# Attention scores as one full product and two 64-row products in different halves of the array

## The chip, the cores and the metric

The kernel runs on one core of a Trainium2 chip. The metric is the device time of one execution in microseconds, the median of several runs. The engines are named as in the profile: PE is TensorE (matrix products; PEld its weight loads), DVE is VectorE, ACT is ScalarE, POOL is GpSimd, and SP is SyncE, whose queue (SPq) issues most DMAs.

## What is computed

One layer of an encoder on 2048 tokens of width 1024, in float32:

```
h  = rms_norm(x); z = h @ W_in -> q_A k_A v_A q_B k_B v_B gate_A gate_B
yA = windowed attention, |t-s| <= 128, 8 query heads on 2 key heads, ALiBi, a sink logit per head
yB = attention in an 8 x 16 neighbourhood of a 32 x 64 token grid, 8 heads, learned bias
x  = x + (sigmoid(gate_A) * (yA @ Wp_A) + sigmoid(gate_B) * (yB @ Wp_B)) @ W_out
x  = x + relu(rms_norm(x) @ W_up)^2 @ W_down
out = rms_norm(x)
```

The head dimension is 64. The scores of both attentions are q . k over these 64 numbers, plus a bias, then a softmax.

## The kernel before

Every float32 operand of a product is split into a rounded high part and a low part (the rest), both in the type float32r. Dense products are three: high times high, high times low, low times high (`mm3`, L199, and `mm3s`, L296).

Scores use another scheme. As a head has only 64 rows, q is stored with its high part in rows 0 to 63 and its low part in rows 64 to 127. The keys are kept twice: once as (high; low) in `k[:, 0]`, once swapped, as (low; high) in `k[:, 1]`. Two products of 128 rows, added in one PSUM bank, then give all four combinations of high and low:

```
PE.matmul(ps[:, :n], q[:, h, :], ka[:, 0, ...], start=True, stop=False)    # L764: hh + ll
PE.matmul(ps[:, :n], q[:, h, :], ka[:, 1, ...], start=False, stop=True)    # L765: hl + lh
```

The stages, in order of time:

- W_in for the first half of the tokens (`in_quad`), with results sent to DRAM. `qk_parts` (L426) splits a result into its parts and returns where they go; the q and k scratch in DRAM are `qs_a`, `qs_b`, `ks_a`, `ks_b`. L464 issues these stores here, L705 for the other half of the tokens, one DMA for each head with both parts.
- Attention A (`attn_a`, L747), 32 units: 2 key heads by 16 blocks of 128 queries. A unit loads its q (L757), makes the scores of 4 heads against up to 384 keys (L764, L765), adds the bias and takes the maximum on DVE (L766), then exponentials on ACT, normalisation on POOL, transposes on PE (L784), and products with v (L789, L790). `load_kv` (L739) loads the keys (L742 to L744).
- Attention B (`attn_b`, L909), 32 units: 8 heads by 4 stripes of columns. A unit has 4 blocks of 128 queries with 288, 384 or 512 keys (L927, two products each), DVE (L932), and the like (transposes at L955, products with v at L967). `load_k` (L900) loads the keys of a head in three DMAs (L904 to L906).
- Between the units of both, the dense products of W_in for the other half of the tokens stand as filler (`feature_tile`, L200 to L202, in `mm3`).
- Then the projections, W_out, the up product and the down product.

PSUM has eight banks in the attention stages: two for `mm` (dense), three for `s` (scores), two for `pt` (transposes), one for `av`. A score takes the next of the three `s` banks and holds it until the DVE pass at L766 or L932 has read it. The order on each engine isn't written out by hand: a scheduler sets it from the dependencies, its estimate of times, and the order in which the program emits the instructions; `issue_after` adds an order by hand in some places, not at the scores.

Of the kernel before, what the change touches and what calls it, by code (L numbers as in the profile page):

```python
# [8 lines left out]
F32 = mybir.dt.float32  # L9
# [13 lines left out]
P = 128  # L23
KC = D // P
NB = 4
BT = 512
# [8 lines left out]
B_R0 = [0, 4, 12, 20]  # L35
B_NR = [12, 16, 16, 12]
B_C0 = [0, 8, 24, 40]
# [55 lines left out]
def encoder_layer(ctx, tc, x, norm_mix, w_in, b_gate, sink, rpb, w_pa, w_pb, w_out,  # L93
                  norm_mlp, w_up, w_down, norm_final, dist_a, mask_b, out):
    nc = tc.nc
    V, A, G, PE, SY = nc.vector, nc.scalar, nc.gpsimd, nc.tensor, nc.sync
# [21 lines left out]
    def psum(tag, bufs):  # L118
        n_ps[0] += 1
        return pps[tag].tile([P, 512], F32, tag=tag, bufs=bufs, name=f"{tag}_{n_ps[0]}")  # L120
# [20 lines left out]
    def flipped(t):  # L141

        (step, n), _ = t.ap
        return bass.AP(t.tensor, t.offset + P - 1, [[step, n], [P, 4], [-16, 8], [-1, 16]])
# [26 lines left out]
    def flush(keep=0, queue=A):  # L171
        while len(pending) > keep:
            queue.dma_start(*pending.pop(0))
# [152 lines left out]
    def zbank(pl, bufs=1):  # L326
        n_ps[0] += 1
        return pl.tile([P, 512], F32, tag="b", bufs=bufs, name=f"zb_{n_ps[0]}")
# [97 lines left out]
    def qk_parts(col, b, src, t2):  # L426

        th, tl = t2[:, 0], t2[:, 1]
        if O_QB <= col < O_VB:
            if col < O_KB:  # L430

                pv = src.rearrange("p (r j c) -> p j r c", r=8, j=4)
                hv, hr, lr = (flipped(t) for t in (th, th.bitcast(F32R), tl.bitcast(F32R)))
            else:

                pv = src.rearrange("p (q r x) -> p q r x", q=2, r=4)
                hv, hr, lr = (t.rearrange("p (q x r) -> p q r x", q=2, r=4)
                              for t in (th, th.bitcast(F32R), tl.bitcast(F32R)))
            A.copy(hr, pv)
            V.tensor_tensor(out=lr, in0=pv, in1=hv, op=ALU.subtract)  # L440
        else:
            scale = 1.0 if col == O_KA else 0.125
            A.activation(th.bitcast(F32R), src, AF.Copy, scale=scale)
            last_low[0] = V.scalar_tensor_tensor(out=tl.bitcast(F32R), in0=src, scalar=scale, in1=th,
                                                 op0=ALU.mult, op1=ALU.subtract).ins
        parts = [(e, t2[e * 64 : e * 64 + 64]) for e in range(2)]
        if col < O_KA:
            dst, h = qs_a[col // 256][b // 2], col // P % 2 * 2
            dst = dst.rearrange("(z p) h i q -> p z h (i q)", z=2)
            return [(dst[:, :, h + e, b % 2 * BT : (b % 2 + 1) * BT], t) for e, t in parts]  # L450
        if O_QB <= col < O_KB:
            dst = qs_b[(col - O_QB) // P]
            return [(dst[e].rearrange("(z p) b j q -> p z b (j q)", z=2)[:, :, b], t) for e, t in parts]
        dst, o = (ks_a[b // 2], b % 2 * BT) if col == O_KA else (ks_b[(col - O_KB) // P], b * BT)
        return [(dst[e].rearrange("(z p) t -> p z t", z=2)[:, :, o : o + BT], t) for e, t in parts]

# [89 lines left out]
    for k in range(KC):  # L546
        ps = zbank(*tbanks[k % 6])
        turned(ps, tiles[0], k)
        h, l = (t[:, k % 4] for t in right[1 + k // 4])
# [22 lines left out]
    for p in range(2):  # L572
        t = T(xp, [P, D], F32, "xin", 8).rearrange("p (k c) -> p k c", k=4)
# [15 lines left out]
    for k in range(KC):  # L589
        ps = zbank(*tbanks[k % 6])  # L590
# [7 lines left out]
        else:  # L598
            h, l = (t[:, kk] for t in right[3])
# [41 lines left out]
    for q in range(2, len(QUADS)):  # L641
# [9 lines left out]
        if q in (5, 6):  # L651

            b = q - 3
# [85 lines left out]
    def load_kv(g, m, behind=None):  # L739
        k, kd = kas[g][:, :, m * (S // 2) : (m + 1) * (S // 2)], ks_a[m][g]  # L740
        with tc.issue_after(behind) if behind else nullcontext():
            SY.dma_start(k[:, 0].bitcast(F32), kd)  # L742
            SY.dma_start(k[0:64, 1].bitcast(F32), kd[64:128])
            SY.dma_start(k[64:128, 1].bitcast(F32), kd[0:64])  # L744
            SY.dma_start(vas[g][:, 8 * m : 8 * m + 8].bitcast(F32), vs_a[m][g])

    def attn_a(g, i):  # L747
        c0, c1 = (1 if i == 0 else 0), (2 if i == 15 else 3)
        lo, hi = c0 * P, c1 * P
        n = hi - lo  # L750
        if bias_a[g] is None:

            with tc.issue_after(shares[2]):
                make_bias_a(g)
        base = (i - 1) * P
        q = T(ap_, [P, 4, P], F32R, "qa", 3)
        began.append(SY.dma_start(q.bitcast(F32), qs_a[g][i // 8][:, :, i % 8]).ins)  # L757
        ka, v = kas[g], vas[g]
        s = T(ap_, [P, 4, 384], F32, "sa", 4)
        st = T(ap_, [P, 8, 4], F32, "sta", 8)  # L760
        mx, nm, sm, es, ri = (st[:, k, :] for k in range(5))
        for h in range(4):
            ps = psum("s", 3)
            PE.matmul(ps[:, :n], q[:, h, :], ka[:, 0, base + lo : base + hi], start=True, stop=False)  # L764
            PE.matmul(ps[:, :n], q[:, h, :], ka[:, 1, base + lo : base + hi], start=False, stop=True)  # L765
            V.tensor_tensor_reduce(out=s[:, h, lo:hi], in0=ps[:, :n], in1=bias_a[g][:, h, lo:hi], scale=1.0,  # L766
                                   scalar=sink_t[:, 4 * g + h : 4 * g + h + 1], op0=ALU.add, op1=ALU.max,
                                   accum_out=mx[:, h : h + 1])
        A.activation(nm, mx, AF.Copy, scale=-1.0)
        V.tensor_tensor(out=es, in0=sink_t[:, 4 * g : 4 * g + 4], in1=mx, op=ALU.subtract)  # L770
        A.activation(es, es, AF.Exp)
        for h in range(4):
            A.activation(s[:, h, lo:hi], s[:, h, lo:hi], AF.Exp, bias=nm[:, h : h + 1], accum_out=sm[:, h : h + 1])
        V.tensor_tensor(out=sm, in0=sm, in1=es, op=ALU.add)
        V.reciprocal(ri, sm)
        for h in range(4):
            share = G.tensor_scalar(s[:, h, lo:hi], s[:, h, lo:hi], ri[:, h : h + 1], 1.0, ALU.mult, ALU.mult)
        shares.append(share.ins)
        yield
        po = psum("av", 1)  # L780
        for c in range(c0, c1):
            pt = psum("pt", 2)
            for h in range(4):
                PE.transpose(pt[:, h * P : (h + 1) * P], s[:, h, c * P : (c + 1) * P], ident)  # L784
            ph = T(ap_, [P, 512], F32R, "ph", 3)
            pl = T(ap_, [P, 512], F32R, "pl", 3)
            A.copy(ph, pt)
            V.tensor_tensor(out=pl, in0=pt, in1=ph.bitcast(F32), op=ALU.subtract)
            PE.matmul(po, v[:, i - 1 + c, :], ph, start=c == c0, stop=False)  # L789
            last = PE.matmul(po, v[:, i - 1 + c, :], pl, start=False, stop=c == c1 - 1).ins  # L790
        done.append(last)
        t = T(ap_, [64, 512], F32, "ya", 2)
        A.copy(t, po[64:128, :])
        V.tensor_tensor(out=t, in0=po[0:64, :], in1=t, op=ALU.add)
        flush(queue=SY)
        put(y_a[g].rearrange("(h d) t -> d h t", d=64)[:, :, i * P : (i + 1) * P],
            t.rearrange("d (h q) -> d h q", h=4))
# [56 lines left out]
    for g in (1, 0):  # L854
        load_kv(g, 0)
# [44 lines left out]
    def load_k(h):  # L900

        k = T(bp, [P, 2, S], F32R, f"kb{h % 2}", 1)
        kd = ks_b[h // 2][h % 2]
        SY.dma_start(k[:, 0].bitcast(F32), kd)  # L904
        SY.dma_start(k[0:64, 1].bitcast(F32), kd[64:128])
        SY.dma_start(k[64:128, 1].bitcast(F32), kd[0:64])  # L906
        return k

    def attn_b(n_u, h, j, k, bias):  # L909
        e, t = h % 2, h // 2  # L910
        w, jt = B_W[j], JT[j]
        kp = 4 * w
        q = T(bp, [P, 4, P], F32R, f"qb{n_u % 3}", 1)
# [6 lines left out]
        mx, nm, sm, ri = (st[:, n, :] for n in range(4))  # L920
        kv = k.rearrange("p z (q f) -> p z q f", q=8)
        s = []
        for i in range(4):
            n = B_NR[i] * w
            ps = psum("s", 3)
            for z in range(2):
                PE.matmul(ps[:, :n], q[:, i, :],  # L927
                          kv[:, z, B_R0[i] // 4 : (B_R0[i] + B_NR[i]) // 4, 4 * B_C0[j] : 4 * (B_C0[j] + w)],
                          start=z == 0, stop=z == 1)
            o = boff[(jt, IT[i])]  # L930
            si = T(bp, [P, 512], F32, f"sb{n_u % 3}", 4)
            V.tensor_tensor_reduce(out=si[:, :n], in0=ps[:, :n], in1=bias[:, o : o + n], scale=1.0, scalar=-3.0e38,  # L932
                                   op0=ALU.add, op1=ALU.max, accum_out=mx[:, i : i + 1])
            s.append(si)
        A.activation(nm, mx, AF.Copy, scale=-0.125)
        for i in range(4):
            n = B_NR[i] * w
# [3 lines left out]
        for i in range(4):  # L941
            n = B_NR[i] * w
# [5 lines left out]
        for pair in range(4):  # L948
            pt = psum("pt", 2)
            at, pieces = 0, []  # L950
# [22 lines left out]
        at = n_u % 2 * 64  # L973
# [363 lines left out]
    for b in range(NB):  # L1337
# [43 lines left out]
        for t in range(4):  # L1381
# [6 lines left out]
            for c in range(2):  # L1388
                xc = xt[:, c * BT : (c + 1) * BT]
                ps = psum("pt", 2)  # L1390
# [245 lines left out]
```

## Time and profile before

| | |
|---|---|
| median of 3 runs | 2621.41 us (2618.64 to 2622.58) |
| the profiled execution, first to last instruction | 2620.1 us |
| mean granted TensorE clock | 0.999 |
| score products of A (L764, L765) | 256, from 361.0 to 622 us |
| score products of B (L927) | 256, from 622.1 to 995 us |
| DMA | 490.30 MB, 187 GB/s |

The profile is of one execution of its own; its span is 1.3 us under the median of the runs. In a row of a group, the count stands after x, then the busy time in us and the mean of one in ns, then the idle time of the engine just before and what ended it. The recorded duration of a product includes the part in which the next one already runs, so durations of neighbours overlap; the distance between starts tells what a product costs in a stream.

### The profile page before, as it was taken

The page shows a single profiled execution, that of the slowest core. Times are in us where ns is not written, and L with a number is a line of the kernel's source. Part 1 is how long each engine was busy: PE and PEld are TensorE (multiplying, and loading weights), DVE is VectorE, ACT ScalarE, POOL GpSimd, SP SyncE. Part 2 cuts the span into 40 slices and gives each one's busy share as a digit, 9 for nine tenths or more (in the row PEclk, how much of TensorE's full clock was granted, in tenths as well). Part 3 has the DMA queues.
Part 4 walks back from the last instruction along what each step waited for, and adds up shares of the span by engine and source line. Part 5 has one row for each costly group of instructions (what it writes and reads, how often), then busy time and mean ns, then how long its engine had stood idle before and what let it go on. Part 6 is the DMA issues. An engine that isn't in the chain of part 4 may idle for free.

```text
span 2620.1 us, 34509 instructions
## 1 busy us (share of the span) xinstructions
PE 2586.9 (99%) x12140; PEld 2149.8 (82%) x12140; DVE 1625.1 (62%) x2653; ACT 1239.8 (47%) x2261; POOL 358.1 (14%) x431
## 2 busy tenths in 40 slices
PE   8999999999999999999999999999999999999999
PEld 6888788778888888888888888888888888888887
DVE  8765666665544444755567777776656534555766
ACT  5335256666555555633334554644544322322454
POOL 1000114344555541000001000100000000000010
PEclk9999999999999999999999999999999999999999
DMA  5657485455876655954556655854428825445555
GB/s 184 200 156 200 141 243 159 114 155 145 240 219 180 191 144 164 318 177 151 179 178 208 245 205 202 302 191 149 153 101 300 300 101 182 146 146 171 183 194 170
DMA packets 353982, 490.30 MB, mean 187 GB/s; under 512 B 28792, under 2 KB 188664, under 8 KB 351632
## 3 DMA queue, kind: packets, MB, share of 16 engines
q1 hardware_dynamic: 346752, 471.04, 56.8%
q10 hardware_dynamic: 7056, 17.04, 1.8%
q8 instruction: 96, 1.57, 0.2%
q14 instruction: 78, 0.64, 0.1%
HBM read 328.54 MB, written 159.45 MB: 186 GB/s over the span
## 4 chain that ended last, share of the span: by engine, by line
PE 88%; DVE 4%; DMA 4%; ACT 2%; issue 1%; SPq 1%; POOL 0%; DVEq 0%; POOLq 0%; ACTq 0%
PE b L297 15%; PE b L299 15%; PE b L298 15%; PE mm L200 6%; PE mm L202 6%; PE mm L201 6%; PE zb L297 3%; PE zb L299 3%; PE zb L298 2%; PE pt L200 2%; PE pt L201 2%; PE pt L202 2%; PE av L967 2%; PE pt L955 2%; PE s L927 2%
## 5 line engine op out<-in xcount | busy, mean ns | idle before, releaser
L298 PE MATMUL b<-dwh,dah 128*128 128x512 f32 x896 | 348.5, 389 | 0.0
L299 PE MATMUL b<-dwh,dah 128*128 128x512 f32 x896 | 347.6, 389 | 0.0
L297 PE MATMUL b<-dwh,dah 128*128 128x512 f32 x896 | 339.6, 389 | 0.0
L293 ACT CAST dah<-da 128x1024 fp32r<-128x1024 f32 (+1 forms) x128 | 120.9, 945 | 368.6 <-PE b L299 241.8
L294 DVE TENSOR_TENSOR dah<-da,dah 128x1024 fp32r<-128x1024 f32 (+1 forms) x128 | 139.7, 1091 | 224.1 <-ACT dah L293 221.1
L297 PE MATMUL b<-ubh,uwhlb 128*128 128x512 f32 x592 | 230.3, 389 | 0.0
L298 PE MATMUL b<-ubh,uwhlb 128*128 128x512 f32 x592 | 230.3, 389 | 0.0
L299 PE MATMUL b<-ubh,uwhlb 128*128 128x512 f32 x592 | 229.3, 389 | 0.1
L200 PE MATMUL mm<-hT,whl 128*128 128x512 f32 x544 | 218.2, 401 | 0.0
L202 PE MATMUL mm<-hT,whl 128*128 128x512 f32 x544 | 215.1, 395 | 0.0
L201 PE MATMUL mm<-hT,whl 128*128 128x512 f32 x544 | 213.7, 393 | 0.0
L298 PEld LDWEIGHTS b<-dwh,dah 128*128 128x128 f32 x896 | 168.2, 188 | 35.0
L299 PEld LDWEIGHTS b<-dwh,dah 128*128 128x128 f32 x896 | 168.2, 188 | 34.9
L297 PEld LDWEIGHTS b<-dwh,dah 128*128 128x128 f32 x896 | 168.2, 188 | 34.9
L297 PE MATMUL zb<-zh,zwhl 128*128 128x512 f32 x476 | 186.7, 394 | 7.9 <-DVE zc L290 3.4
L298 PE MATMUL zb<-zh,zwhl 128*128 128x512 f32 x476 | 186.4, 392 | 0.0
L299 PE MATMUL zb<-zh,zwhl 128*128 128x512 f32 x476 | 183.7, 392 | 0.3 <-DVE zwhl L294 0.3
L290 DVE TENSOR_TENSOR uc<-b,uc 128x512 f32<-128x512 f32 x160 | 109.2, 689 | 104.2 <-PE b L299 103.2
L1506 POOL TENSOR_TENSOR st<-st,power 128x1 f32<-128x1 f32 x16 | 13.3, 841 | 925.0 <-DVE st L1505 924.9
L297 PEld LDWEIGHTS b<-ubh,uwhlb 128*128 128x128 f32 x592 | 111.1, 188 | 23.8 <-issue 0.4
L299 PEld LDWEIGHTS b<-ubh,uwhlb 128*128 128x128 f32 x592 | 111.1, 188 | 23.5 <-DVE uwhlb L294 0.5
L298 PEld LDWEIGHTS b<-ubh,uwhlb 128*128 128x128 f32 x592 | 111.1, 188 | 23.1
(253 smaller groups left out, 5912.5 us busy)
## 6 DMA issues: line engine op xcount, KB each, us to landing
at<-uc SPq DMA_DIRECT2D x224, 256.0 KB, 2.0
da<-at SPq DMA_DIRECT2D x96, 512.0 KB, 3.7
dw<-in_w_down_dram SPq DMA_DIRECT2D x160, 256.0 KB, 4.8
uraw<-in_w_up_dram SPq DMA_DIRECT2D x32, 1024.0 KB, 6.8
raw<-in_w_in_dram SPq DMA_DIRECT2D x34, 512.0 KB, 4.7
zraw<-in_w_in_dram SPq DMA_DIRECT2D x16, 1024.0 KB, 7.7
z<-zg SPq DMA_DIRECT2D x64, 256.0 KB, 5.1
qa<-qs_a SPq DMA_DIRECT2D x32, 256.0 KB, 8.3
```

What stands on the lines that cost most here:

```text
L200: PE.matmul(ps, lh, rh, start=first, stop=False)
L201: PE.matmul(ps, lh, rl, start=False, stop=False)
L202: PE.matmul(ps, ll, rh, start=False, stop=last)
L290: return eng.tensor_tensor(out=out, in0=a, in1=b, op=op).ins
L293: A.copy(hi, src)
L294: return eng.tensor_tensor(out=lo, in0=src, in1=hi.bitcast(F32), op=ALU.subtract).ins
L297: PE.matmul(ps, lh, rh, start=first, stop=False, skip_group_check=True)
L298: PE.matmul(ps, lh, rl, start=False, stop=False, skip_group_check=True)
L299: PE.matmul(ps, ll, rh, start=False, stop=last, skip_group_check=True)
L927: PE.matmul(ps[:, :n], q[:, i, :], kv[:, z, B_R0[i] // 4 : (B_R0[i] + B_NR[i]) // 4, 4 * B_C0[j] : 4 * (B_C0[j] + w)], start=z == 0, stop= ...
L955: PE.transpose(pt[:kp, at + (i - i0) * P : at + (i - i0 + 1) * P], s[i][:, rr : rr + kp], ident)
L967: last = PE.matmul(po[:, i0 * P : (i0 + ni) * P], v[:kp, c, :], src[:kp, o : o + ni * P], start=first, stop=(c == 7 and z == 1), skip_grou ...
```

## The change

Low times low is left out. What is left is (high + low) of q times high of k, and high of q times low of k. The first is one product of 128 rows when the keys have their high part in both halves of the partitions. The second needs 64 rows only. The keys are now loaded as (high; high) in `k[:, 0]` and (low; low) in `k[:, 1]`, in two DMAs. The queries of odd heads in A, and of odd blocks in B, are stored turned, (low; high), so that their high part lies in rows 64 to 127; their stores become two DMAs of half the size. The program emits the scores two by two: two full products into two banks, then the two 64-row products, rows 0 to 63 for the first and 64 to 127 for the second, with the DVE passes behind them. The number of products stays the same, 12140 in all. In the changed program the full and the 64-row product are at L776 and L779 (A), and at L947 and L951 (B).

```diff
@@ qk_parts @@
         parts = [(e, t2[e * 64 : e * 64 + 64]) for e in range(2)]
+
+        def placed(dst, t, turn):
+
+            return [(dst[:, 1 - z], t[:, z]) for z in range(2)] if turn else [(dst, t)]
+
+        out = []
         if col < O_KA:
             dst, h = qs_a[col // 256][b // 2], col // P % 2 * 2
             dst = dst.rearrange("(z p) h i q -> p z h (i q)", z=2)
-            return [(dst[:, :, h + e, b % 2 * BT : (b % 2 + 1) * BT], t) for e, t in parts]
+            for e, t in parts:
+                out += placed(dst[:, :, h + e, b % 2 * BT : (b % 2 + 1) * BT], t, e == 1)
+            return out
         if O_QB <= col < O_KB:
             dst = qs_b[(col - O_QB) // P]
-            return [(dst[e].rearrange("(z p) b j q -> p z b (j q)", z=2)[:, :, b], t) for e, t in parts]
+            for e, t in parts:
+                out += placed(dst[e].rearrange("(z p) b j q -> p z b (j q)", z=2)[:, :, b], t, b % 2 == 1)
+            return out
@@ load_kv, and the same in load_k @@
-            SY.dma_start(k[:, 0].bitcast(F32), kd)
-            SY.dma_start(k[0:64, 1].bitcast(F32), kd[64:128])
-            SY.dma_start(k[64:128, 1].bitcast(F32), kd[0:64])
+            for e in range(2):
+                SY.dma_start(k[64 * e : 64 * e + 64].bitcast(F32), kd.rearrange("(z p) t -> p z t", z=2))
@@ attn_a @@
+        scores = {}
         for h in range(4):
-            ps = psum("s", 3)
-            PE.matmul(ps[:, :n], q[:, h, :], ka[:, 0, base + lo : base + hi], start=True, stop=False)
-            PE.matmul(ps[:, :n], q[:, h, :], ka[:, 1, base + lo : base + hi], start=False, stop=True)
+            if h % 2 == 0:
+                for e in range(2):
+                    scores[h + e] = psum("s", 3)
+                    PE.matmul(scores[h + e][:, :n], q[:, h + e, :], ka[:, 0, base + lo : base + hi], start=True, stop=False)
+                for e in range(2):
+                    at = slice(64 * e, 64 * e + 64)
+                    PE.matmul(scores[h + e][:, :n], q[at, h + e, :], ka[at, 1, base + lo : base + hi], start=False, stop=True)
+            ps = scores[h]
@@ attn_b @@
+        scores = {}
+
+        def keys(at, z, i):
+            return kv[at, z, B_R0[i] // 4 : (B_R0[i] + B_NR[i]) // 4, 4 * B_C0[j] : 4 * (B_C0[j] + w)]
+
         for i in range(4):
             n = B_NR[i] * w
-            ps = psum("s", 3)
-            for z in range(2):
-                PE.matmul(ps[:, :n], q[:, i, :],
-                          kv[:, z, B_R0[i] // 4 : (B_R0[i] + B_NR[i]) // 4, 4 * B_C0[j] : 4 * (B_C0[j] + w)],
-                          start=z == 0, stop=z == 1)
+            if i % 2 == 0:
+                for x in range(2):
+                    scores[i + x] = psum("s", 3)
+                    PE.matmul(scores[i + x][:, : B_NR[i + x] * w], q[:, i + x, :], keys(slice(0, P), 0, i + x),
+                              start=True, stop=False)
+                for x in range(2):
+                    at = slice(64 * x, 64 * x + 64)
+                    PE.matmul(scores[i + x][:, : B_NR[i + x] * w], q[at, i + x, :], keys(at, 1, i + x),
+                              start=False, stop=True)
+            ps = scores[i]
```

More of the change, by code (lines that the diff above doesn't have):

```diff
@@ L903, in load_k @@
         kd = ks_b[h // 2][h % 2]
-        SY.dma_start(k[:, 0].bitcast(F32), kd)
-        SY.dma_start(k[0:64, 1].bitcast(F32), kd[64:128])
-        SY.dma_start(k[64:128, 1].bitcast(F32), kd[0:64])
+        for e in range(2):
+            SY.dma_start(k[64 * e : 64 * e + 64].bitcast(F32), kd.rearrange("(z p) t -> p z t", z=2))
         return k
```

## The prediction

> **What bounds the kernel now.** I read the page first, for the engine that fills the span.
>
> ```profile
> span 2620.1 us, 34509 instructions
> PE 2586.9 (99%) x12140; PEld 2149.8 (82%) x12140; DVE 1625.1 (62%) x2653; ACT 1239.8 (47%) x2261; POOL 358.1 (14%) x431
> ...
> PE 88%; DVE 4%; DMA 4%; ACT 2%; issue 1%; SPq 1%; POOL 0%; DVEq 0%; POOLq 0%; ACTq 0%
> ```
>
> TensorE (PE) is busy 99% of the span and carries 88% of the chain that ended last. A busy PE can still hide bubbles, so the next question is where the change sits and whether PE is also the limit there. The first score product of attention A has this row in the view of its line; attention B (L927) follows from 622 us:
>
> ```profile
> L764 PE MATMUL s<-ka,qa x128: 274/339/446, 361.0 to 621.8; 128*128 128x384 f32 x112, 128*128 128x256 f32 x16
> ```
>
> The view by windows gives the two stretches:
>
> ```profile
> core 0: us, PE busy (x) PEld busy (x) DVE busy (x) ACT busy (x) POOL busy (x), PEclk, DMA share, GB/s
> ...
> 361.00:622.00 261.00, 254.99 (x1313) 209.06 (x1313) 170.64 (x479) 169.89 (x456) 102.14 (x146) 1.00 0.57 157
> 622.00:1000.00 378.00, 375.71 (x2154) 326.18 (x2152) 181.49 (x467) 212.89 (x516) 196.19 (x217) 1.00 0.68 189
> ```
>
> PE is busy 98% and 99% of them at full clock, VectorE (DVE) 65% and 48%. What PE saves or loses on scores is saved or lost in the end time. The groups by line and shape name the products concerned:
>
> ```profile
> L764 PE MATMUL s<-ka,qa 128*128 128x384 f32 x112 | 41.5, 370 | 1.4 <-DVE sta L766 1.3
> L765 PE MATMUL s<-ka,qa 128*128 128x384 f32 x112 | 37.7, 337 | 0.0
> L927 PE MATMUL s<-kb,qb 128*128 128x384 f32 x128 | 33.4, 353 | 0.7 <-DVE stb L932 0.7
> L927 PE MATMUL s<-kb,qb 128*128 128x512 f32 x64 | 19.1, 405 | 0.2 <-DVE stb L932 0.2
> L927 PE MATMUL s<-kb,qb 128*128 128x288 f32 x64 | 15.3, 314 | 1.0 <-DMA kb<-ks_b 1.0
> L766 DVE CUSTOM_DVE_ANT_0 sa<-s,biasa,sink_t 128x384 f32<-128x384 f32 x112 | 64.7, 612 | 25.0 <-PE pt L784 14.9 <-PE s L765 8.2 <-POOL sa L777 1.5
> ```
>
> The mean of one product (337 to 405 ns) isn't its price, because products overlap in the pipeline. The price is the distance from start to start, which the timeline of PE shows (start, duration, line):
>
> ```profile
> 485.22 0.39 PE L200 MATMUL mm<-hT,whl 128*128 128x512 f32 x1
> 485.45 0.39 PE L201 MATMUL mm<-hT,whl 128*128 128x512 f32 x1
> 485.68 0.39 PE L202 MATMUL mm<-hT,whl 128*128 128x512 f32 x1
> 485.90 0.38 PE L784 MATMUL pt<-ident,sa 128*128 128x128 f32 x2
> 486.04 0.48 PE L789 MATMUL av<-ph,va 128*128 128x512 f32 x1
> 486.36 0.39 PE L790 MATMUL av<-pl,va 128*128 128x512 f32 x1
> 486.58 0.82 PE L784 MATMUL pt<-ident,sa 128*128 128x128 f32 x6
> 487.16 0.42 PE L764 MATMUL s<-ka,qa 128*128 128x384 f32 x1
> 487.42 0.34 PE L765 MATMUL s<-ka,qa 128*128 128x384 f32 x1
> 487.59 0.34 PE L764 MATMUL s<-ka,qa 128*128 128x384 f32 x1
> 487.77 0.33 PE L765 MATMUL s<-ka,qa 128*128 128x384 f32 x1
> 488.23 0.44 PE L764 MATMUL s<-ka,qa 128*128 128x384 f32 x1
> 488.51 0.34 PE L765 MATMUL s<-ka,qa 128*128 128x384 f32 x1
> 488.69 0.40 PE L789 MATMUL av<-ph,va 128*128 128x512 f32 x1
> ```
>
> Three products of 512 columns take 0.68 us (485.22 to 485.90), 0.227 us each; one of 384 takes 0.17 us (487.42 to 487.59). That is 0.44 ns per column, whatever the line.
>
> **The change part by part.** *What it would take away.* Two neighbouring scores cost four products now; afterwards two full ones and two of 64 rows in different halves of the array. If each pair of halves ran at once, the shorter of the two would be free. In A that is 56 pairs of 384 columns and 8 of 256 (the first row of L764 has 112 and 16 products of these widths): (56 x 384 + 8 x 256) x 0.44 ns = 10.4 us. In B each pair is (288, 384) or (384, 512), 32 of each: (32 x 288 + 32 x 384) x 0.44 ns = 9.5 us. Together 19.9 us, the most this can bring.
>
> *What the built program does.* Two halves run at once only if they follow each other on PE, and the diff doesn't settle that: a scheduler orders the engine. The order of PE's instructions in the changed program has, in attention A:
>
> ```
> L776 Matmult s_88<-ka1,qa 128x384
> L779 Matmult s_88<-ka1,qa 128x384
> L776 Matmult s_89<-ka1,qa 128x384
> L779 Matmult s_89<-ka1,qa 128x384
> ```
>
> L776 is the full product, L779 the half; s_88 and s_89 are the two scores of one pair. The half of a score stands right behind its own full product, not beside its partner. Of 128 pairs just 5 stand together (4 in A, 1 in B). But for eight moves by a place or two, PE's order is that of the old program with each second product replaced. The reason is the ring of three score banks: a full product needs a bank, and 248 of the 256 stand behind a wait, while no half does. A bank comes free when the DVE pass over an older score ends, and the L766 row has 0.61 us for one; the first score's half is ready well before the second score's bank. So of 19.9 us the order leaves 5 pairs, at most 5 x 0.17 = 0.8 us.
>
> *What a half costs by itself.* It streams the same columns. Fewer rows make no product shorter, as the products of 96 and of 128 rows show:
>
> ```profile
> L967 PE MATMUL av<-phb,vb 96*128 96x256 f32 x96 | 27.8, 304 | 0.1
> L967 PE MATMUL av<-phb,vb 128*128 128x256 f32 x96 | 27.4, 299 | 0.2 <-ACT phb L960 0.2
> ```
>
> So 0 us each way, which excludes a gain from this side.
>
> *What it adds: 502 changes of array form.* Every product of before uses the array whole. Now 256 use a half, and since they stand alone, PE goes from whole to half and back 502 times (248 in A, 254 in B). No row of before has such a change; I bound it. Below: nothing. The nearest row is a change between transposes and products: from 485.90 to 487.42 run 8 transposes, two products of 512 and one of 384. A transpose takes (0.82 - 0.27) / 5 = 0.11 us (the x6 row, one alone lasting 0.27), so 0.88 + 0.454 + 0.17 = 1.504 of 1.52 us, and four such changes cost 0.016 us, under 0.01 us each. Above: a product whose weight load couldn't run ahead, as after the wait at 488.23, holds PE 0.28 us in place of 0.17, so 0.11 us. Waiting for the last results of the product before would cost its duration less its distance, 0.39 - 0.227 = 0.16 us; both together 0.27 us. Times 502: 0, 5, 55, 80 and 136 us. A transpose changes what passes through the array, not how its rows are divided, so I take its price as too low, and 0.16 us, a whole pipeline emptied, as too high for a first guess; between 0.01 and 0.16 the middle in ratio is 0.04 us: 502 x 0.04 = 20 us. This is a choice, and the range keeps the ends.
>
> The Trainium skill speaks against the change here: "TensorEngine Tiling (Array Packing)", section "Key Properties", says that a change of tiling mode, as against a change of tile, drains TensorE. It gives no duration; no run here shows one yet. By it the sum would lie at the upper prices.
>
> *DMAs.* Half of the q stores become two of half the size (32 more issues), and each load of k takes two issues in place of three (12 fewer): 20 more on SyncE's queue. The views of two of these tiles, the waits of SyncE's queue and those of PE:
>
> ```profile
> L705 SPq DMA_DIRECT2D qs_a<-z x16: 574/598/1267, 417.1 to 488.1; - x16
> L906 SPq DMA_DIRECT2D kb<-ks_b x8: 581/595/1070, 578.3 to 909.3; - x8
> ```
>
> ```profile
> SPq L757 <- PE s L765: 55.7, 20, 6.7
> ```
>
> ```profile
> PE s L927 <- DMA kb<-ks_b: 1.0, 1, 1.0
> ```
>
> An issue takes 0.6 us, 20 of them 12 us of SyncE in some 870 us. Behind such a store stand loads of weights, q and v. SyncE itself waits 55.7 us for PE at the q loads (L757), and PE waited for a score load once, 1.0 us. That slack hides it: 0 us; without it a load comes 0.6 us later, some 2 us in all. Bytes stay the same. ScalarE keeps its order, DVE and GpSimd but for three swaps.
>
> *Sum.* 2620.1 + 20 - 0.8 = 2639.3 us against the profiled span. The median of the runs, 2621.41, lies 1.3 us above that span; carried along, 2640.6: **2641 us**.
>
> **The rivals.**
>
> 1. *A change of form costs no more than between transposes and products* (0 to 0.02 us): 2621 + (0 to 10) - 0.8, thus 2620 to 2630 us. For it: the 0.016 us over four changes above, and weight loads that run ahead. Against: none of those divides rows. This is the case on the other side: up to 0.012 us a change (6 us less 0.8) the time stays within 0.2%, 5.2 us, about what a measurement here can tell from no change.
> 2. *Each change empties the array*: 0.16 us x 502 = 80 us, 2701 us; with the weight load exposed as well, 136 us, 2757 us. For it: scores accumulate in one bank across two forms, so the second must not overtake the first. Against: at 486.04 and 487.16 products enter at once behind transposes.
> 3. *The pairs run at once all the same*: 2621 - 20 = 2602 us if changes of form are free. It needs the halves to stand together, and 123 of 128 pairs don't. It decides only if PE could hold back one half and let a whole product pass; the rows show products starting in their program's order throughout.
>
> The Trainium skill's page "TensorE: Matmul & The Clock Gate", Part 3 ("Packing small matmuls"), reports 3.07 times the speed for four row tiles at once, which is the rule behind the third; it also has matmuls start strictly in order, which agrees with the timeline here and leaves that gain to neighbours alone.
>
> **How the numbers follow.** The forecast, 0.02 to 0.09 us a change (2631 to 2666 us), 0.40. Rival 1, 0.34: 0.26 within 0.2% and 0.08 just above. Rival 2 with all beyond 0.09 us, 0.22. Rival 3, 0.04. So faster 0.04, same 0.26, slower 0.70. The range runs from 2618 (rival 1 with its run-to-run scatter) to 2703 (the emptied array): it leaves out rival 3 and about half of rival 2, some 0.14.
>
> **What would show it.** In the timeline after: L776 followed by L779 at 0.17 us for 384 columns means a free change, 0.21 the forecast, 0.33 an emptied array; likewise from L779 to whatever follows. The stretches of both attentions lengthen, 10 us each; all after 1000 us is the same, shifted. Two halves starting some hundredths of a us apart should be seen at 5 places only; seen at 128, my reading of the order is wrong. DVE waiting longer for scores (L766 on PE) would be the effect of a slower PE, not a cause; PE waiting for a DMA at scores would prove the SyncE step wrong.

## The result and the profile after

The changed kernel takes 2709.07 us in the median (2706.48 to 2712.09), the kernel before 2621.99 us (four runs of each): 1.0335 times the time, 95% interval 1.0322 to 1.0348, or 87 us more. The forecast was slower, 2641 us, with a range that ended at 2703.

The page of the changed kernel has the same bound:

```profile
span 2710.3 us, 34581 instructions
PE 2677.8 (99%) x12140; PEld 2157.1 (80%) x12140; DVE 1625.6 (60%) x2653; ACT 1241.5 (46%) x2261; POOL 357.8 (13%) x431
```

The span is 90 us longer, and PE's busy time is 91 us longer with the same 12140 products. The busy times of DVE, ACT and POOL stand within 2 us of before. The windows now laid around the two attentions (score products from 363.7 to 664 us and from 664.7 to 1086 us) hold the same products as the windows of before, but for two in each:

```profile
363.00:664.00 301.00, 297.92 (x1311) 213.80 (x1311) 172.60 (x481) 170.85 (x456) 101.93 (x146) 0.98 0.52 137
664.00:1090.00 426.00, 423.03 (x2152) 327.58 (x2150) 179.84 (x464) 212.86 (x514) 194.79 (x217) 1.00 0.64 167
```

Attention A went from 261 to 301 us, attention B from 378 to 426 us: 88 of the 90 us. Where it goes inside is seen in the timeline of PE (start, duration, line), L776 being the full product and L779 the half:

```profile
500.16 0.40 PE L202 MATMUL mm<-hT,whl 128*128 128x512 f32 x1
500.40 0.33 PE L776 MATMUL s<-ka,qa 128*128 128x384 f32 x1
500.66 0.44 PE L779 MATMUL s<-ka,qa 64*128 64x384 f32 x1
501.03 0.50 PE L804 MATMUL av<-ph,va 128*128 128x512 f32 x1
501.37 0.39 PE L805 MATMUL av<-pl,va 128*128 128x512 f32 x1
501.60 0.60 PE L799 MATMUL pt<-ident,sa 128*128 128x128 f32 x4
```

and in that of the weight loads over the same stretch:

```profile
500.16 0.19 PEld L776 LDWEIGHTS s<-ka,qa 128*128 128x128 f32 x1
500.66 0.18 PEld L779 LDWEIGHTS s<-ka,qa 64*128 64x128 f32 x1 [0.31 <-issue]
501.03 0.19 PEld L804 LDWEIGHTS av<-ph,va 128*128 128x128 f32 x1 [0.19 <-issue]
501.14 0.19 PEld L805 LDWEIGHTS av<-pl,va 128*128 128x128 f32 x1
```

The full product is followed after 0.26 us where 384 columns take 0.17 (the prediction had named 0.21 us here as the sign of its forecast and 0.33 us as that of an emptied array): 0.09 us are lost. The half is followed after 0.37 us: 0.20 lost. The product behind it, of 512 columns, is followed after 0.34 us where 0.227 is usual: 0.11 lost. The weight loads tell why. In a stream a load starts with the product before its own: that of L776 at 500.16, with L202. The half's load starts at 500.66, only when the half itself starts, and likewise that of L804 at 501.03, behind the half. In front of both PEld stands idle until "issue", that is without a wait for any semaphore that the profile shows. This reads as follows: at each change of form, in either direction, nothing of the next product, not even its weights, enters until the last one has left: 0.09 us until then, and 0.11 us for a weight load that is no longer hidden. The starts show both lengths; that the array is empty in between is inferred, as the ends of products in the record are modelled. A load and its product start together in the record, so the 0.11 us show up in the longer duration of the product (0.44 in place of 0.33 us).

The order was as read: among the starts of all products, 5 pairs of halves stand together, 3 ns apart; the other 246 halves stand alone.

### The profile page after: what moved, and what is told of

Same layout as the page of the kernel before. It is cut to its first block, busy times and chain, and to the rows that moved or that the text cites. A ratio compares the mean times of both kernels' runs of the same rounds, so it can differ in the third digit from the quotient of the medians.

```text
span 2710.3 us, 34581 instructions
## 1 busy us (share of the span) xinstructions
PE 2677.8 (99%) x12140; PEld 2157.1 (80%) x12140; DVE 1625.6 (60%) x2653; ACT 1241.5 (46%) x2261; POOL 357.8 (13%) x431
## 4 chain that ended last, share of the span: by engine, by line
PE 91%; DVE 4%; DMA 3%; issue 1%; ACT 1%; SPq 1%; POOL 0%; DVEq 0%; POOLq 0%; ACTq 0%
PE b L297 14%; PE b L299 14%; PE b L298 14%; PE mm L202 6%; PE mm L200 6%; PE mm L201 6%; PE zb L297 3%; PE zb L299 3%; PE zb L298 3%; PE av L991 2%; PE pt L200 2%; PE pt L201 2%; PE pt L202 2%; PE pt L979 2%; PE s L951 2%; PE s L779 2%
## 5 line engine op out<-in xcount | busy, mean ns | idle before, releaser
L200 PE MATMUL mm<-hT,whl 128*128 128x512 f32 x544 | 220.8, 406 | 0.0
L202 PE MATMUL mm<-hT,whl 128*128 128x512 f32 x544 | 218.6, 402 | 0.0
L201 PE MATMUL mm<-hT,whl 128*128 128x512 f32 x544 | 216.2, 397 | 0.0
```

The lines of the kernel that those rows point to most:

```text
L200: PE.matmul(ps, lh, rh, start=first, stop=False)
L201: PE.matmul(ps, lh, rl, start=False, stop=False)
L202: PE.matmul(ps, ll, rh, start=False, stop=last)
```

## The experiments

The theory after the result: the loss is 502 changes of form at some 0.2 us in a stream, less where PE waited anyway. Rivals: the loss is a price of each 64-row product; the new stores, loads or the emission two by two carry a part; the chip doesn't run neighbours in different halves at once. Of each kernel the median is given and, behind "before", that of the kernel before on the same chip.

### full_rows and paired_full_rows: the change without a change of form

```diff
-                    at = slice(64 * e, 64 * e + 64)
+                    at = slice(0, P)
```

in both attentions. PE, DVE, ACT and POOL keep the order of the changed kernel.

> The changed kernel with its second products over all 128 rows: same order on every engine, same stores and loads, no change of array form; low times low is computed again, in the same product. Theory (all of the loss is the 502 changes of form, about 0.2 us each): 2622 us, like before. Rival (stores, loads or the two-by-two emission carry a part): between 2630 and 2709 us; all of it, 2709 us.

Measured: 2628.36 us, before 2622.73 (1.0021, 1.0012 to 1.0031). Of 87 us, 81.5 go with the form of 256 products, in the same order, with the same stores and loads. With the 0.8 us of the 5 pairs that makes 82.3 / 502 = 0.164 us for a change on the average. The rival has 5.6 us, which the last experiments follow up.

As the order on PE is the same in both traces, the distance from each product to the next can be set side by side. In the median it grows by 0.09 us at the 178 full products before a half, by 0.19 at the 246 lone halves, by 0.10 at the 178 full products behind a half and by 0.19 at the 73 between two halves. The 11453 products away from a change grow by nothing in the median and by 2.8 us in all, of the 85.7 us between these two traces. The average of 0.164 us lies under the 0.20 of a stream because some of the changes fall where `full_rows` loses time as well: of the 178 products behind a half, 41 lose under 0.06 us, and 29 of these already lose some 0.11 us or more in `full_rows`.

In `paired_full_rows` the second products are moved behind the second full product of the pair (the order of `paired`, below).

> As paired in order, with second products over all 128 rows: no change of form. It shows what the new order alone costs. Theory: 2622 us, at most 5 us above (halves wait for the second score bank). Rival (the order with two full products first makes PE wait for banks): 2630 us or more.

Measured: 2623.37 us, before 2622.73 (1.0004, 0.9995 to 1.0013). That order by itself costs nothing; the ring of three banks bears it. These 0.6 us include the new stores and loads, which `full_rows` has too.

### paired and paired_same_half: halves side by side

```diff
+                    full = PE.matmul(scores[h + e][:, :n], q[:, h + e, :], ka[:, 0, ...], start=True, stop=False)
...
+                    with tc.issue_after(full.ins):
+                        PE.matmul(scores[h + e][:, :n], q[at, h + e, :], ka[at, 1, ...], start=False, stop=True)
```

> The changed kernel with each pair's 64-row products held behind the second full product, so that 127 of 128 pairs stand together: 258 changes of form in place of 502. Theory (a price per change, 0.175 to 0.197 us; neighbours in different halves run at once, 19.7 us): 2622 + 45 to 51 - 20 = 2647 to 2653 us. Rival 1 (the price is per 64-row product, 0.35 us each): 2622 + 88 - 20 = 2690 us. Rival 2 (the chip runs such neighbours one after the other in a kernel): 2667 to 2673 us.

Measured: 2650.30 us, before 2622.73 (1.0106, 1.0091 to 1.0121).

In `paired_same_half` all queries are stored unturned and `at = slice(0, 64)` holds for both heads or blocks.

> As paired, but both 64-row products in rows 0 to 63 (queries not turned): same order on PE, 258 changes of form, nothing that can run at once. Theory: paired plus the 19.7 us of running at once, 2667 to 2673 us. Rival (neighbours in one half cost a change as well): 2690 us or more.

Measured: 2664.46 us (1.0169, 1.0152 to 1.0186). The timeline of PE in `paired` (a row with x2 merges two neighbours):

```profile
560.18 0.33 PE L776 MATMUL s<-ka,qa 128*128 128x384 f32 x1
560.44 0.44 PE L780 MATMUL s<-ka,qa 64*128 64x384 f32 x2
560.81 0.45 PE L776 MATMUL s<-ka,qa 128*128 128x384 f32 x1
```

and in `paired_same_half`:

```profile
563.54 0.33 PE L776 MATMUL s<-ka,qa 128*128 128x384 f32 x1
563.80 0.62 PE L780 MATMUL s<-ka,qa 64*128 64x384 f32 x2
564.35 0.44 PE L776 MATMUL s<-ka,qa 128*128 128x384 f32 x1
```

Two halves in different halves of the array take 0.37 us from start to the next product, as one does alone; in the same half 0.55 us. So neighbours run at once, weight loads included, and the gain of 0.18 us a pair is real: 20 us over 127 pairs in the distances. The medians show 14 us of it. Some 6 us return elsewhere in the attentions: the granted clock is half for 10.2 us in `paired` (393.1 to 396.5 and 690.1 to 696.9 us) and for 3.4 us in `paired_same_half` (698.3 to 701.7 us), a difference of some 3 us in time, and PE isn't busy for 7.5 us of the attentions (361 to 1045 us) against 5.2 (361 to 1060 us).

The price: 2664.46 - 2623.37 = 41.1 us for 258 changes, 0.159 us each, close to the 0.164 of 502. `paired_same_half` and the changed kernel both have 256 halves; a price of each half would have left 81 us. That rival has fallen.

### a_only: one attention

Attention B with its loads and products as before, attention A changed.

> The change in attention A alone, attention B as before: 248 changes of form, 4 pairs together. Theory (0.16 us a change, as between full_rows and the changed kernel): 2623 + 40 - 1 = 2662 us, all of it gained between 361 and 660 us. Rival (the two attentions push each other's loads and waits): clearly off half of the loss, under 2650 or over 2680 us.

Measured: 2662.74 us, before 2620.35 (1.0163, 1.0148 to 1.0178). 42.4 us, half of the loss with half of the changes. Attention B takes as long as before: its score products start over 373 us in both (663.9 to 1037.2 us, before 622.3 to 995.3).

### down_one_half, down_two_halves and down_pairs: the price by itself

For n = 2 of the down product (the edit of `down_one_half`; in `down_two_halves` the third product is over rows 0 to 63 too; in `down_pairs` the halves of two neighbouring banks stand side by side, in different halves of the array; the rows left out of the sum are left out of the result):

```diff
-                mm3s(banks[t], lh, ll, rh, rl, ...)
+                PE.matmul(banks[t], lh, rh, ...)
+                PE.matmul(banks[t], lh[0:64], rl[0:64], ...)
+                PE.matmul(banks[t], ll, rh, ...)
```

> The kernel before, and in one seventh of the down product (the group of 8 banks by 16 steps for n = 2) high times low over rows 0 to 63 alone, the other 64 rows of that term left out: 128 64-row products of 512 columns in a stream without waits, 256 changes of form. Theory (0.09 us to empty the array and 0.107 us for the weight load that can't run ahead, 0.197 us a change): 2623 + 50 = 2673 us. Rival (the loss belongs to the scores' accumulation or to their waits): 2623 us.

Measured: 2673.55 us, before 2620.35 (1.0202, 1.0185 to 1.0219). There are no scores in this stretch, PE waits for no other engine and no DMA, and the trace shows the bare pattern:

```profile
2199.67 0.39 PE L1581 MATMUL b<-dwh,dah 128*128 128x512 f32 x1
2199.99 0.18 PEld L1582 LDWEIGHTS b<-dwh,dah 64*128 64x128 f32 x1 [0.35 <-issue]
2199.99 0.50 PE L1582 MATMUL b<-dwh,dah 64*128 64x512 f32 x1
2200.42 0.19 PEld L1583 LDWEIGHTS b<-dwh,dah 128*128 128x128 f32 x1 [0.24 <-issue]
2200.42 0.50 PE L1583 MATMUL b<-dwh,dah 128*128 128x512 f32 x1
2200.53 0.19 PEld L1581 LDWEIGHTS b<-dwh,dah 128*128 128x128 f32 x1
2200.75 0.39 PE L1581 MATMUL b<-dwh,dah 128*128 128x512 f32 x1
```

Three products of 512 columns take 1.08 us in place of 0.68: 0.32, 0.43 and 0.33 us. A change to the half and back costs 0.40 us, 0.20 us a change; times 256 that is 51 us, and the spans differ by 2670.9 - 2620.1 = 50.8 us. The medians differ by 53.2 us, with 48 to 57 in the interval.

> As down_one_half, but low times high is a 64-row product too, right behind the other and in the same half (rows 64 to 127 of both terms left out): 256 64-row products, but 254 changes of form as before. Theory (price per change): 2673 us, like down_one_half. Rival (price per 64-row product, 0.39 us each): 2623 + 100 = 2723 us.

Measured: 2674.27 us, before 2620.35 (1.0203, 1.0188 to 1.0218). Twice the halves, the same changes, the same time. The timeline of PE, L1582 and L1583 being the halves:

```profile
2199.55 0.50 PE L1582 MATMUL b<-dwh,dah 64*128 64x512 f32 x1
2199.89 0.39 PE L1583 MATMUL b<-dwh,dah 64*128 64x512 f32 x1
2200.21 0.49 PE L1581 MATMUL b<-dwh,dah 128*128 128x512 f32 x1
2200.64 0.50 PE L1582 MATMUL b<-dwh,dah 64*128 64x512 f32 x1
```

0.34 and 0.32 and 0.43 us: the second half has its weights early again (duration 0.39), and the 0.40 us fall once, at the way in and the way out.

> As down_one_half in what it computes of each bank (64 rows of high times low, rows 0 to 63 for even banks and 64 to 127 for odd ones), with two banks at a time: four full products, then the two 64-row ones in different halves; 136 changes of form, 59 pairs right beside each other. Theory (0.197 us a change, neighbours at once): 2623 + 27 - 13 = 2637 us. Rival (neighbours don't run at once here): 2650 us.

Measured: 2636.91 us, before 2620.35 (1.0062, 1.0047 to 1.0077). That is 16.6 us more, 12 to 20 in the interval, where the sum of the theory is 14.

```profile
2200.18 0.40 PE L1598 MATMUL b<-dwh,dah 128*128 128x512 f32 x1
2200.50 0.49 PE L1602 MATMUL b<-dwh,dah 64*128 64x512 f32 x2
2200.93 0.50 PE L1597 MATMUL b<-dwh,dah 128*128 128x512 f32 x1
```

The pair takes 0.43 us, as one half did: two at once here too, saving 0.227 us at a price of 0.40.

### The other 5 us: full_rows_again, full_rows_loads4, stores_only, loads_only

In `full_rows` the loss of 4 us stands at one place. PE waits for the keys of B's second head, and then runs slower for a while:

```profile
682.31 0.37 PE L947 MATMUL s<-kb,qb 128*128 128x288 f32 x1 [3.63 <-DMA kb<-ks_b]
682.52 0.30 PE L951 MATMUL s<-kb,qb 128*128 128x288 f32 x1
682.65 0.60 PE L409 MATMUL mm<-ident,z 128*128 128x128 f32 x4
683.01 0.48 PE L200 MATMUL mm<-hT,whl 128*128 128x512 f32 x1
683.32 0.40 PE L201 MATMUL mm<-hT,whl 128*128 128x512 f32 x1
683.55 0.54 PE L202 MATMUL mm<-hT,whl 128*128 128x512 f32 x1
683.89 0.63 PE L200 MATMUL mm<-hT,whl 128*128 128x512 f32 x1
684.32 0.52 PE L947 MATMUL s<-kb,qb 128*128 128x384 f32 x1
```

The wait is 3.6 us (1.0 us before), and behind it 512 columns take 0.43 us in place of 0.227; the granted clock in 683.6 to 687.1 us is 0.51. At half the clock 3.4 us lose another 1.7.

```diff
             for e in range(2):
-                SY.dma_start(k[64 * e : 64 * e + 64].bitcast(F32), kd.rearrange("(z p) t -> p z t", z=2))
+                for z in range(2):
+                    SY.dma_start(k[64 * e : 64 * e + 64, z].bitcast(F32), kd[64 * z : 64 * z + 64])
```

> full_rows once more, beside the next kernel: 5 to 6 us above before (2626 to 2628 us).

Measured: 2627.64 us, before 2622.92 (1.0017, 1.0009 to 1.0026).

> full_rows with each load of keys as four DMAs, one for each quarter of the tile (64 partitions, one of the two copies), in place of two. In full_rows the keys of B land 12.8 us after issue against 10.1 us before, and PE waits 3.6 us for them once against 1.0 us. Theory (the shape of the key loads makes them late, and that is the 5 us): keys land near 10 us, 2622 to 2624 us. Rival (the 32 additional store issues, or chance in the order, make them late): 2626 to 2628 us as full_rows.

Measured: 2628.59 us (1.0020, 1.0011 to 1.0029), the wait still 3.4 us. Four loads are no better than two, so the number of pieces isn't it. Two more kernels part the stores from the loads: `stores_only` is `full_rows` with the three loads of keys of before (a full second product takes either layout), `loads_only` is `full_rows` with `placed(..., False)` for all queries.

> full_rows with the keys loaded as before (three DMAs); the turned queries and their 32 additional stores stay. Theory (the stores, on the queue and in the DMA engines around the key load of B at 667 us, make that load late): 2626 to 2628 us and the one wait for keys over 3 us. Rival (the loads over 64 partitions are the slow ones): 2622 to 2624 us, wait near 1 us.

Measured: 2622.11 us, before 2622.53 (1.0000, 0.9991 to 1.0009).

> full_rows with the queries stored as before (not turned, no additional stores); the new loads of keys stay, two DMAs each. Theory (the stores are the cause): 2622 to 2624 us, wait near 1 us. Rival (the loads over 64 partitions): 2626 to 2628 us, wait over 3 us.

Measured: 2627.43 us, before 2622.53 (1.0018, 1.0009 to 1.0027). The waits of PE, first in `stores_only`, then in `loads_only`:

```profile
PE s L953 <- DMA kb<-ks_b: 0.9, 1, 0.9
```

```profile
PE s L947 <- DMA kb<-ks_b: 4.0, 1, 4.0
```

My theory for these two had the stores at fault, and it fell: the loads are the cause. The 32 added stores cost nothing; key loads that each cover 64 partitions make the 5 us in this order, in two pieces or in four. The landings named in the expectation of `full_rows_loads4` (12.8 and 10.1 us) are medians of the only 2 and 5 loads whose landing is on record, and not of this one. For this one the time from the issue of the load to the product that waits for it tells: 10.7 us before (667.40 to 678.07 us) and in `stores_only`, and 13.2 to 13.7 us in `full_rows` (669.12 to 682.31 us), `full_rows_again`, `full_rows_loads4`, `loads_only` and the changed kernel.

What the later keys cost depends on the order. `paired_full_rows` has the same loads; PE waits 2.6 us at the same head (the profile puts the wait down to another DMA), no stretch at half clock follows, and the kernel is only 0.6 us above before. The stretch from 667 to 683 us, in the kernel before and in `loads_only` (the last three columns are clock, DMA share and GB/s):

```profile
667.00:683.00 16.00, 14.48 (x85) 12.30 (x84) 9.80 (x28) 9.19 (x25) 10.60 (x10) 1.00 0.96 256
```

```profile
667.00:683.00 16.00, 11.22 (x65) 9.32 (x63) 7.61 (x22) 10.07 (x26) 8.71 (x8) 0.95 0.81 186
```

The two stretches don't begin at the same work, as the load is issued at 667.4 us in the one and at 669.4 us in the other. In the 10.7 us behind the issue it is 251 GB/s before, 253 in `stores_only` and 188 in `loads_only`, with the DMA engines busy alike (0.91, 0.91 and 0.90). Why these loads move less isn't settled; the loads of before mix one piece over 128 partitions with two over 64.

## Why the prediction was wrong, point by point

- **PE is the bound in both attentions.** Right: the other engines' work is unchanged, and PE's added time is the added span.
- **The order leaves 5 of 128 pairs together, so nearly nothing is gained.** Right. With the pairs together (`paired`) 20 us come back in the distances and 14 in the time, near the 19.7 expected. That such pairs run at once is shown by their 0.37 us against 0.55 in the same half; their starts lie 3 ns apart.
- **A half costs what its columns cost.** Right: in the same form, 512 columns of a half take 0.32 to 0.34 us with one lost 0.09 or 0.11 in it, thus 0.23.
- **502 changes of form at 0.04 us.** This is the step that failed. The mechanism and the count were right, the price was not: 0.16 us a change in the attentions (0.164 and 0.159), 0.20 in a stream. I set aside both upper rows, the 0.11 us of a weight load that can't run ahead and the 0.16 us of an emptied pipeline, and took a middle between them and the changes between transposes and products. Those keep the form and tell nothing of its change. What was measured is the mechanism of rival 2 with the weight load exposed: the array emptied, for which 0.09 us is the price and not 0.16 (the 0.16 came from the recorded end of a product, which is modelled), and the weight load, 0.11 us as the row had it. With the sizes of the prediction, 0.27 us together, it gave 2757 us, too much. That the rival's first figure, 0.16 us and 2701 us, lies within 8 us of the result is luck: it counted the emptying alone, and the measured average of 0.164 is the 0.20 of both, less what PE would have lost anyway.
- The Trainium skill's sentence on this ("TensorEngine Tiling (Array Packing)", "Key Properties") agrees with every run here: a change of mode drains TensorE, and a change of tile within the mode (`paired`) shows no such loss. The page gives no number; these runs give 0.20 us in a stream.
- **"Every product of before uses the array whole."** Wrong, and rows of 96 shown in the prediction itself (L967) say so: the kernel before has 256 products of 96 rows and 128 changes between 96 and 128 rows. They cost nothing. A 96-row product of 256 columns is followed by a 128-row one after 0.12 us, as by another of 96 rows, and 384 columns of a whole product are followed by a 96-row one after 0.17 us, here in `full_rows`:

```profile
676.98 0.28 PE L991 MATMUL av<-phb,vb 96*128 96x256 f32 x1
677.10 0.49 PE L979 MATMUL pt<-ident,sb 128*96 128x128 f32 x3
...
677.61 0.34 PE L951 MATMUL s<-kb,qb 128*128 128x384 f32 x1
677.78 0.28 PE L991 MATMUL av<-plb,vb 96*128 96x256 f32 x1
```

So fewer rows alone make no change of form here; 64 rows do. This row would have argued for too low a price.

- **DMAs at nothing.** Wrong by 5 us in the order of the changed kernel. I reckoned the issues on SyncE's queue, which cost nothing (`stores_only`), and said that the bytes stay the same; the loads over 64 partitions brought them later, at the one place where PE already waited 1.0 us for keys. The row was in the prediction, read as slack when it was the sign of none.
- **Not foreseen: the clock.** The granted clock fell to half for 3.4 us at four more places within the attentions, as here:

```profile
441.80:445.20 3.40, 3.40 (x13) 2.59 (x13) 0.70 (x4) 2.51 (x9) 3.21 (x6) 0.50 1.13 223
...
602.20:605.60 3.40, 3.40 (x11) 2.13 (x10) 1.03 (x3) 2.97 (x9) 2.20 (x4) 0.50 0.73 182
```

Four times 3.4 us at half the clock are at most 6.8 us of the 87: three of them contained in the 0.16 us above, the one at 728.5 us, behind PE's wait of 2.4 us for keys, in the 5 us of the loads. The changes alone don't bring it. The 3.4 us in front of each of the three hold six to eight score products and a wait of 0.3 to 0.4 us for DVE, and by an estimate from their starts the columns of all products, at 0.44 ns each, fill 0.44 to 0.47 of the time. In `down_one_half` the columns fill 0.68 of 1.08 us, 0.63, and the clock stays whole over 256 changes (1.00 from 2178 to 2316 us). How sparse a stretch must be isn't settled: one of the changed kernel at 622.7 us, filled to 0.47 as well, isn't followed by half a clock. The Trainium skill ("TensorE: Matmul & The Clock Gate", Part 1) has the clock at half after an idle window of about 3.4 us. Length and height agree; the 3.4 us in front of the three weren't idle.

No version here beats the kernel before. A trip into the other form and back costs 0.40 us in a stream, and a pair of 384 columns saves 0.17. By these two numbers three pairs a trip would pay, 0.51 against 0.40 us. They would hold six score banks, and the kernel has three; this wasn't tried.

## What to carry to other kernels

Products over 64 of the array's rows pay only in company: count the changes of form in the order that the scheduler really makes, at 0.2 us each in a stream, before counting columns saved. Where a price isn't in the trace, ask which rows lie next to it in mechanism and add them up, rather than splitting the difference; here "array emptied" and "weights not ahead" together were the answer, at 0.09 and 0.11 us, though the first was over-sized in the prediction. And a load for which the bound engine already waits a little has no slack, however idle the queue that issues it.

## What the runs showed of the hardware

- Between whole-array and 64-row products PE loses 0.09 us, both ways, which reads as the array emptying, and the next weight load, 0.11 us, is exposed. Between 128 and 96 rows it loses nothing. Within the 64-row form, two products in different halves start 3 ns apart, and two in the same half follow each other with the second's weights loaded ahead.
- Short stalls together with waits bring the clock down: four windows of 3.4 us at half clock in the changed kernel's attentions, where the kernel before has none in its own; one wait of 3.6 us does it as well. The changes alone, in a stream that the columns fill to 0.63, don't.
- Keys loaded over 64 partitions at a time reached the product that waited for them 13.2 to 13.7 us after issue, by the mixed loads of before 10.7 us, with the DMA engines as busy (0.90 and 0.91) and fewer bytes moved (188 and 251 GB/s).
